# Context steps dealt out anew among the expert sets, and the column tiles of a round issued in reverse

## The chip, the core and the metric

The kernel runs on one core of one Trainium2 chip. The metric is the device time of one execution in microseconds (us); of the kernel before, three runs and one further, profiled execution are known. TensorE (PE in the rows) multiplies, its weight loads are PEld; VectorE is DVE, ScalarE is ACT, GpSimd is POOL, and SP is SyncE, whose queue issues nearly all loads from HBM. TensorE's clock has two levels, 1.2 and 2.4 GHz; a granted clock of 1.00 in the rows means 2.4 GHz all the time.

## The reference, cut to what matters

Two transformer blocks on 256 tokens of width 1024, in float32. The first block ends in a mixture of 32 experts, of which each token uses four. The second block has two layers; it works on the tokens and on a second stream of 256 context rows. The context stream of layer 0 needs nothing of the first block.

```
def moe_ffn(h, router_w, router_b, w1, b1, w2, b2):
    logits = (xt @ router_w + router_b)
    top_v, top_e = lax.top_k(logits, TOP_K)
    ...
    def expert_block(args):
        xblk, e = args
        act = clamped_swiglu(xblk @ w1[e] + b1[e])
        return act @ w2[e] + b2[e]

def second_block(x, c, ctx, ...):
    for l in range(DEPTH_2):
        ...
        y, yc = token_mixer(h, hc, rope, need_ctx, ...)
        xl = xl + gt1 * rms_norm(y, g_post_mix[l])
        ...
        if need_ctx:
            xc = xc + cgt1 * rms_norm(yc, g_post_mix[l])
            hc = rms_norm(xc, g_pre_ffn[l]) * (1.0 + csc2) + csh2
            xc = xc + cgt2 * rms_norm(swiglu(hc, w_ffn_in[l], w_ffn_out[l]), g_post_ffn[l])
```

The weights of one expert are w1 (1024 x 2048) and w2 (1024 x 1024), 12.6 MB together; all 32 experts are read, 403 MB.

## The kernel before, in words

The program is written as generators. `run` drives the first block, then the experts (`moe`), and beside the experts a second generator, `cside`: layer 0 of the context stream, cut into steps. A step takes one tile `raw` of 1 MB of weights from HBM, cuts its two halves into a high and a low part (`split`: ACT writes `wh` at L363, DVE writes `wl` at L364) and issues 48 matmuls on 256 columns into the PSUM bank `ps_c` (`fm` at L384 to L386, `tm` at L407 to L409, `tm2` at L433 to L435). What the step's result needs (attention, a convolution, norms, gates) follows in the same step or is spread over the next ones.

The experts are sorted by their number of tokens and worked in twelve sets: four quads (four experts, 32 column places each, list `QUADS`), six pairs (two experts of 64 places) and two mixed sets (96 and 32 places, cut into four column tiles of 32 by `w`). A column tile is a part of TensorE's columns with a stationary operand of its own (`xg`, the gathered tokens) and the PSUM partitions that belong to it; the expert's weights are the moving operand. A set has 24 rounds: eight k steps for each half `hf` of w1 (L1154, into `ps_a`) and eight for w2 (L1179, into `ps_b`). In a round each column tile (`parts`) gets two matmuls of 512 columns; in the trace each of them is two records. A round of a quad needs 2 MB of weights, loaded as four transfers of 512 KB (L1129) into two tiles `raw`; a pair or a mixed set loads whole tiles of 1 MB for each expert (L1118) and makes two rounds of them, so that a round needs 1 MB. A set ends with the matmuls at L1198, which bring its result to `acc`.

What sets the order: each round ends with `yield credit`, and `drive` adds the credits up; whenever the sum reaches 1, one context step is issued at that place of the program. The context stream may run to 74 steps here (`CTX_STEPS - REST`); then nothing more is dealt out. Behind the program's own order a scheduler decides how the instructions that are near each other stand on each engine; every engine, and the queue of SP, then works strictly in that order. Two rings of buffers matter: the seven tiles of 1 MB for the experts' weights (`RAW = 7`) and a ring of its own for the context's weights while the experts run (`rawx`), which holds one tile; so a context load can't be issued before the step ahead of it has been split.

Of the kernel before, what the change touches and what calls it, by code (L numbers as in the profile page):

```python
# [28 lines left out]
for _s in SETS:  # L29
    for _r, _o, _m in _s:  # L30
        CAPS[_r] = _m
CREDIT = {1: 0.0, 2: 0.5, 4: 0.4}
NEG = 1e30
HEADS = 16
CONVW = 31
# [257 lines left out]
class _Kernel:  # L293
# [839 lines left out]
    def experts(self, tp, rawp, es, rs, xg, b1, sel, ct, acc, mid=None, first=None):  # L1133

        V, S, T, A = self.V, self.S, self.T, self.A
        n = len(es)
        parts = []

        w = 32 if any(m != rs[0][2] for _, _, m in rs) else rs[0][2]
        for i, (_, o, m) in enumerate(rs):  # L1140
            parts += [(slice(c, c + w), i) for c in range(o, o + m, w)]
        credit = CREDIT[n] if n == 4 else CREDIT[n] / 2
        aT = tp.tile([128, 8, 128], F32, name="aT", tag="aT", bufs=1)
        for hf in range(2):
            pg = self.bank("a")
            pl = self.bank("a")
            for j, ps in enumerate((pg, pl)):
                T.matmul(ps, sel[:, 2 * hf + j], b1, start=True, stop=False)
            k = 0
            for kc in range(4):  # L1150
                for ws in self.weights(rawp, A["w1"], es, hf * 4 + kc):
                    for ps, o in ((pg, 0), (pl, 512)):
                        for c, i in parts:
                            T.matmul(ps[c], xg[:, k, c], ws[i][:, o:o + 512],  # L1154
                                     start=False, stop=(k == 7), tile_position=(0, c.start))
                    k += 1
                    if k < 8:
                        yield credit
            t = tp.tile([128, 512], F32, name="et", tag="et", bufs=1)
            g, l = pg, pl  # L1160
            V.tensor_scalar(g, pg, 7.0, None, op0=OP.min)  # L1161
            S.activation(t, g, AF.Tanh, scale=0.851)  # L1162
            V.tensor_scalar(l, pl, 7.0, -7.0, op0=OP.min, op1=OP.max)
            V.scalar_tensor_tensor(t, t, 1.0, g, op0=OP.add, op1=OP.mult)
            V.scalar_tensor_tensor(t, l, 1.0, t, op0=OP.add, op1=OP.mult)
            pt = self.pst()
            for f in range(4):
                T.transpose(pt[:, f * 128:(f + 1) * 128], t[:, f * 128:(f + 1) * 128], self.ident)
            S.activation(aT[:, hf * 4:hf * 4 + 4, :], pt.rearrange("p (f n) -> p f n", f=4), AF.Copy, scale=0.5)
            yield credit  # L1170
        if mid is not None:
            mid()
        py = [self.bank("b") for _ in range(2)]
        f = 0
        for fc in range(4):
            for ws in self.weights(rawp, A["w2"], es, fc):
                for h in range(2):
                    for c, i in parts:
                        T.matmul(py[h][c], aT[:, f, c], ws[i][:, h * 512:(h + 1) * 512],  # L1179
                                 start=(f == 0), stop=(f == 7), tile_position=(0, c.start))  # L1180
                f += 1
                if f < 8:
                    yield credit
        y = tp.tile([128, 1024], F32, name="ey", tag="aT", bufs=1)
        for h in range(2):
            S.activation(y[:, h * 512:(h + 1) * 512], py[h], AF.Copy)
        for a in range(2):
            for h in range(2):
                ps = self.pst()
                hs = slice(h * 512, (h + 1) * 512)  # L1190
                if first is not None:

                    gT, (b2,) = first
                    T.matmul(ps, gT[:, a * 128:(a + 1) * 128], b2[0:NE, hs], start=True, stop=False)
                    T.matmul(ps, ct[:, a, :], y[:, hs], start=False, stop=True)
                    S.activation(acc[:, a, hs], ps, AF.Copy)
                    continue
                T.matmul(ps, ct[:, a, :], y[:, hs], start=True, stop=True)  # L1198
                V.tensor_add(acc[:, a, hs], acc[:, a, hs], ps)
        yield credit  # L1200
# [662 lines left out]
```

## Time and profile before

| | before |
|---|---|
| median of 3 runs | 2876.57 us (2874.08 to 2879.45) |
| profiled execution, its own time | 2880.69 us |
| its span, first to last instruction | 2878.9 us |
| PE, PEld, DVE, ACT busy | 94%, 70%, 50%, 38% of the span |
| mean granted clock | 0.981 |
| read from HBM | 780.74 MB, 274 GB/s over the span |

The busy shares are means over stages with different limits, and a busy TensorE holds time in which a matmul record covers a wait behind it. What the change can be worth is therefore read set by set, between the ends of the twelve expert sets, which lie between 367 and 1725 us.

### The profile page before, as it was taken

To read this page: it belongs to the slowest core of one execution; us is meant where nothing else is said; L and a number is where in the kernel's file an instruction comes from. 1 tells how busy PE (TensorE), PEld (TensorE's weight loads), DVE (VectorE), ACT (ScalarE), POOL (GpSimd) and SP (SyncE) were. 2 spreads that over 40 slices of the span, in tenths; PEclk is the share of its full clock that TensorE was granted. 3 is DMA by queue.
4 is the path that set the end of the run, shared out by engine and by line. 5 is a ranking of instruction groups with operands and counts; after the bars stand their busy time and mean duration, and the time that the engine had idled before them with its cause. 6 is when DMAs were issued, how large, how long until landed. Compare 5 with 4: busy or idle time off the path is not lost. (4 is left out here: it accounts for less than half of the span.)

```text
span 2878.9 us, 47309 instructions
## 1 busy us (share of the span) xinstructions
PE 2710.6 (94%) x19078; PEld 2022.1 (70%) x19078; DVE 1439.7 (50%) x2413; ACT 1093.0 (38%) x1970; POOL 194.8 (7%) x305
## 2 busy tenths in 40 slices
PE   6999999989899999999999998999999999999998
PEld 4888854555554556555655337788989997889998
DVE  3974653253223333323332116886665658866655
ACT  3653522322123222212221115555644455556443
POOL 1110100000000000000000002220000021300000
PEclk8999999989999999999999999999999999999999
DMA  8768678999999998888788996445766563345452
GB/s 335 265 264 331 236 274 317 343 349 397 378 392 358 396 366 326 336 330 323 311 338 337 405 413 229 147 161 211 252 221 234 201 214 125 113 159 183 156 189 74
DMA packets 145406, 790.94 MB, mean 275 GB/s; under 512 B 16832, under 2 KB 18880, under 8 KB 78112
## 3 DMA queue, kind: packets, MB, share of 16 engines
q1 hardware_dynamic: 141056, 773.46, 70.4%
q0 software_dynamic: 4128, 14.42, 1.3%
q8 instruction: 151, 2.47, 0.3%
q14 instruction: 71, 0.58, 0.1%
HBM read 780.74 MB, written 7.08 MB: 274 GB/s over the span
## 5 line engine op out<-in xcount | busy, mean ns | idle before, releaser
L364 DVE TENSOR_TENSOR wl<-raw,wh 128x1024 fp32r<-128x1024 f32 (+1 forms) x542 | 653.9, 1219 | 550.2 <-ACT wh L363 533.2
L363 ACT ACTIVATE wh<-raw 128x1024 fp32r<-128x1024 f32 (+1 forms) x542 | 558.9, 1047 | 656.0 <-PE ps_a L385 311.4
L384 PE MATMUL ps_a<-hh,wh 128*128 128x256 f32 x1888 | 543.3, 288 | 7.2 <-ACT wh L363 3.9
L385 PE MATMUL ps_a<-hl,wh 128*128 128x256 f32 x1888 | 532.7, 282 | 0.4 <-DVE hl L534 0.2
L386 PE MATMUL ps_a<-hh,wl 128*128 128x256 f32 x1888 | 532.5, 282 | 0.6 <-DVE wl L364 0.6
L1154 PE MATMUL ps_a<-raw,xg 128*32 128x512 f32 (+1 forms) x2304 | 441.1, 599 | 3.8 <-DMA raw<-in_w_dram 3.6
L384 PEld LDWEIGHTS ps_a<-hh,wh 128*128 128x128 f32 x1888 | 359.3, 190 | 53.7 <-issue 37.7
L385 PEld LDWEIGHTS ps_a<-hl,wh 128*128 128x128 f32 x1888 | 359.1, 190 | 3.0 <-DVE wl L364 1.4
L386 PEld LDWEIGHTS ps_a<-hh,wl 128*128 128x128 f32 x1888 | 358.7, 190 | 3.1 <-DVE wl L364 2.6
L1154 PEld LDWEIGHTS ps_a<-raw,xg 128*32 128x32 f32 (+1 forms) x2304 | 124.2, 119 | 243.4 <-issue 211.6
L384 PE MATMUL ps_c<-hh,wh 128*128 128x256 f32 x832 | 246.4, 296 | 17.4 <-ACT wh L363 17.2
L386 PE MATMUL ps_c<-hh,wl 128*128 128x256 f32 x832 | 245.7, 295 | 11.3 <-DVE wl L364 11.3
L385 PE MATMUL ps_c<-hl,wh 128*128 128x256 f32 x832 | 238.9, 287 | 0.0
L1179 PE MATMUL ps_b<-raw,aT 128*32 128x512 f32 (+1 forms) x1152 | 215.4, 597 | 1.0 <-DMA raw<-in_w_dram 1.0
L384 PEld LDWEIGHTS ps_c<-hh,wh 128*128 128x128 f32 x832 | 162.3, 195 | 53.0 <-ACT wh L363 35.2
L386 PEld LDWEIGHTS ps_c<-hh,wl 128*128 128x128 f32 x832 | 162.4, 195 | 37.3 <-DVE wl L364 26.2
L385 PEld LDWEIGHTS ps_c<-hl,wh 128*128 128x128 f32 x832 | 162.3, 195 | 5.3 <-issue 5.3
L1677 DVE SCALAR_TENSOR_TENSOR wv<-u,cw,wv 128x256 f32<-128x256 f32 x360 | 163.9, 496 | 1.3 <-ACT wv L1674 0.7
L1179 PEld LDWEIGHTS ps_b<-raw,aT 128*32 128x32 f32 (+1 forms) x1152 | 59.7, 118 | 115.8 <-issue 105.1
L1161 DVE TENSOR_SCALAR ps_a<-ps_a 128x512 f32<-128x512 f32 x24 | 16.8, 700 | 193.8 <-PE ps_a L1154 193.8
L454 PE MATMUL ps_c<-raw,st 128*32 128x512 f32 x576 | 84.2, 608 | 2.1 <-DMA raw<-in_w_ada_dram 2.1
L1162 ACT ACTIVATE et<-ps_a 128x512 f32<-128x512 f32 x24 | 14.3, 597 | 189.0 <-DVE ps_a L1161 188.9
(506 smaller groups left out, 4486.8 us busy)
## 6 DMA issues: line engine op xcount, KB each, us to landing
raw<-in_w_dram SPq DMA_DIRECT2D x384, 512.0 KB, 10.3
raw<-in_w_dram SPq DMA_DIRECT2D x192, 1024.0 KB, 9.4
raw<-in_w_in_dram SPq DMA_DIRECT2D x120, 1024.0 KB, 5.1
raw<-in_w_f_dram SPq DMA_DIRECT2D x66, 1024.0 KB, 4.9
raw<-in_w_mod_dram SPq DMA_DIRECT2D x48, 1024.0 KB, 5.7
raw<-in_w_ada_dram SPq DMA_DIRECT2D x24, 1024.0 KB, 8.4
raw<-in_w_y_dram SPq DMA_DIRECT2D x24, 1024.0 KB, 6.3
raw<-in_w_f2a_dram SPq DMA_DIRECT2D x24, 1024.0 KB, 4.9
```

Of the source, the lines that this page charges most:

```text
L363: s = self.S.activation(h[:, :n], src, AF.Copy)
L364: self.V.tensor_sub(l[:, :n], src, h[:, :n].bitcast(F32))
L384: self.T.matmul(o, wh[:, w], ah, start=(k == 0), stop=False)
L385: self.T.matmul(o, wh[:, w], al, start=False, stop=False)
L386: self.T.matmul(o, wl[:, w], ah, start=False, stop=(k == kt - 1))
L454: self.T.matmul(ps[32 * j:32 * j + 32, :], st[:, k, :], raw[:, 512 * j:512 * (j + 1)], start=(k == 0), stop=(k == 7), tile_position=(0, 32 ...
L1154: T.matmul(ps[c], xg[:, k, c], ws[i][:, o:o + 512], start=False, stop=(k == 7), tile_position=(0, c.start))
L1161: V.tensor_scalar(g, pg, 7.0, None, op0=OP.min)
L1162: S.activation(t, g, AF.Tanh, scale=0.851)
L1179: T.matmul(py[h][c], aT[:, f, c], ws[i][:, h * 512:(h + 1) * 512], start=(f == 0), stop=(f == 7), tile_position=(0, c.start))
L1677: return V.scalar_tensor_tensor(wk, u[:, f, j:j + 256], cw[:, j * 4 + k:j * 4 + k + 1], wk, op0=OP.mult, op1=OP.add)
```

## The change

Two things in `experts` and the table above it. The credit of a round was 0.4 in a quad and 0.25 in a pair or mixed set (`CREDIT[2] / 2`); it is now 0.6 and 0.07. And the list of a round's column tiles is reversed, so that the tile whose expert's weights are loaded last is issued first.

```
-CREDIT = {1: 0.0, 2: 0.5, 4: 0.4}
+CREDIT = {1: 0.0, 2: 0.07, 4: 0.6}
...
         for i, (_, o, m) in enumerate(rs):
             parts += [(slice(c, c + w), i) for c in range(o, o + m, w)]
-        credit = CREDIT[n] if n == 4 else CREDIT[n] / 2
+
+        parts.reverse()
+        credit = CREDIT[n]
```

How it moves instructions, first on ACT, in the third quad, from the Tanh of the first half of w1 (L1162, two lines lower in the changed kernel) to that of the second half, eight rounds later. Before:

```order
L1162 ACTIVATE et<-ps_a 128x512
L363 ACTIVATE wh<-raw 128x1024
L1169 ACTIVATE aT<-ps_t 128x512
L363 ACTIVATE wh<-raw 128x1024 x3
L1416 ACTIVATE tg<-ps_c,hbg 128x256 x2
L363 ACTIVATE wh<-raw 128x1024 x2
L1416 ACTIVATE tg<-ps_c,hbg 128x256 x2
L1162 ACTIVATE et<-ps_a 128x512
```

The same place in the changed kernel, where the context stream is at later steps:

```order
L1164 ACTIVATE et<-ps_a 128x512
L363 ACTIVATE wh<-raw 128x1024 x2
L1171 ACTIVATE aT<-ps_t 128x512
L1418 ACTIVATE tg<-ps_c,hbg 128x256 x2
L363 ACTIVATE wh<-raw 128x1024 x2
L1418 ACTIVATE tg<-ps_c,hbg 128x256 x2
L363 ACTIVATE wh<-raw 128x1024 x2
L1563 ACTIVATE mh<-m 128x512 x4
L363 ACTIVATE wh<-raw 128x1024 x2
L557 ACTIVATE rjk,rst<-ps_c 128x256 x2
L363 ACTIVATE wh<-raw 128x1024 x2
L557 ACTIVATE rjk,rst<-ps_c 128x256 x2
```

Six splits, the weights of three context steps, stand between the two halves before, and ten, those of five steps, in the change.

On ACT in one of the later pairs, `aT` and `et` being the expert's own work and `ah`, `fs`, `y` the context's feed-forward. A stretch of a pair before, from behind one set's end to the second half's transpose:

```order
L363 ACTIVATE wh<-raw 128x1024 x2
L1365 ACTIVATE y<-ps_c 128x2x256
L1162 ACTIVATE et<-ps_a 128x512
L363 ACTIVATE wh<-raw 128x1024 x2
L1169 ACTIVATE aT<-ps_t 128x512
L1343 ACTIVATE fs<-ps_c 128x512
L363 ACTIVATE wh<-raw 128x1024 x2
L1348 ACTIVATE ah<-fs 128x512
L1162 ACTIVATE et<-ps_a 128x512
L363 ACTIVATE wh<-raw 128x1024 x2
L1169 ACTIVATE aT<-ps_t 128x512
```

A whole pair of the change, from the first half's Tanh to the set's end (L1188):

```order
L1164 ACTIVATE et<-ps_a 128x512
L1171 ACTIVATE aT<-ps_t 128x512
L363 ACTIVATE wh<-raw 128x1024 x2
L1164 ACTIVATE et<-ps_a 128x512
L1171 ACTIVATE aT<-ps_t 128x512
L1094 ACTIVATE xg<-ps_t,modT,A_3548 128x128 x8
L1188 ACTIVATE ey<-ps_b 128x512 x2
```

Where a pair had the splits of four steps in the rows of two thirds of it, it now has those of one in the whole.

On PE in a quad, where a context step begins (`oh`, `hh` are the step's activations). Before:

```order
L1154 MATMUL ps_a<-raw,xg 32x512 x23
L384 MATMUL ps_c<-oh,wh 128x256
L385 MATMUL ps_c<-ol,wh 128x256
L1154 MATMUL ps_a<-raw,xg 32x512
L386 MATMUL ps_c<-oh,wl 128x256
L384 MATMUL ps_c<-oh,wh 128x256
```

In the change:

```order
L386 MATMUL ps_c<-hh_8578,wl 128x256
L1156 MATMUL ps_a<-raw,xg 32x512 x16
L384 MATMUL ps_c<-hh_8578,wh 128x256
L385 MATMUL ps_c<-hl_8579,wh 128x256
L386 MATMUL ps_c<-hh_8578,wl 128x256
```

The scheduler drew the first column tile of the next round, whose weights come first, into the context step, away from the other seven matmuls of its round; reversed, the rounds stand whole (16 is two rounds of eight).

## Rows read from the trace of the kernel before

**Rows 1.** Windows, one for each expert set (four quads, six pairs, two mixed).

```profile
core 0: us, PE busy (x) PEld busy (x) DVE busy (x) ACT busy (x) POOL busy (x), PEclk, DMA share, GB/s
367.00:565.00 198.00, 189.58 (x1046) 102.75 (x1044) 76.59 (x192) 60.09 (x158) 9.35 (x14) 0.97 0.90 324
565.00:720.00 155.00, 137.94 (x920) 83.86 (x920) 67.70 (x136) 43.93 (x91) 3.52 (x8) 0.93 0.97 366
720.00:883.00 163.00, 152.12 (x943) 88.97 (x942) 43.39 (x61) 32.46 (x50) 11.17 (x22) 0.96 1.01 387
883.00:1054.00 171.00, 154.85 (x979) 92.88 (x978) 55.56 (x77) 46.53 (x77) 1.54 (x3) 0.98 0.96 375
1054.00:1152.00 98.00, 91.65 (x522) 54.78 (x522) 35.03 (x58) 29.22 (x51) 2.56 (x5) 0.98 0.81 330
...
1442.00:1539.00 97.00, 92.52 (x540) 56.49 (x540) 29.45 (x41) 21.78 (x32) 0.75 (x2) 1.00 0.81 327
1539.00:1604.00 65.00, 61.31 (x298) 28.43 (x296) 13.69 (x25) 7.12 (x15) 0.74 (x2) 1.00 0.91 368
1604.00:1666.00 62.00, 57.92 (x442) 21.87 (x442) 8.19 (x14) 6.49 (x14) 0.75 (x2) 1.00 1.00 412
1666.00:1725.00 59.00, 53.74 (x407) 17.91 (x405) 8.69 (x13) 6.39 (x10) 0.00 (x0) 1.00 1.01 417
```

**Rows 2.** The same windows, ACT's splits at L363 alone: the four quads.

```profile
367.00:565.00 198.00, 14.98 (x15) 0.97 0.90 324
565.00:720.00 155.00, 19.86 (x20) 0.93 0.97 366
720.00:883.00 163.00, 18.15 (x18) 0.96 1.01 387
883.00:1054.00 171.00, 22.22 (x22) 0.98 0.96 375
```

**Rows 3.** The same windows, matmuls into `ps_c` alone: the last two pairs.

```profile
1442.00:1539.00 97.00, 38.15 (x288) 1.00 0.81 327
1539.00:1604.00 65.00, 6.22 (x48) 1.00 0.91 368
```

**Rows 4.** DMA of the four quads, 367 to 1054 us: total, and one issue line.

```profile
DMA packets 62513, 248.28 MB, mean 361 GB/s; under 512 B 6975, under 2 KB 6975, under 8 KB 57311
...
raw<-in_w_in_dram SPq DMA_DIRECT2D x23, 1024.0 KB, 10.3
```

**Rows 5.** PE's timeline in the third quad: start, us, instructions.

```profile
731.69 1.04 PE L1154 MATMUL ps_a<-raw,xg 128*32 128x512 f32 x2
732.67 0.39 PE L386 MATMUL ps_c<-hh,wl 128*128 128x256 f32 x1
```

**Rows 6.** PE's timeline in the first quad.

```profile
393.27 1.90 PE L1154 MATMUL ps_a<-raw,xg 128*32 128x512 f32 x4
...
440.36 1.92 PE L1154 MATMUL ps_a<-raw,xg 128*32 128x512 f32 x8
```

**Rows 7.** PE's timeline in a pair.

```profile
1182.57 7.09 PE L1154 MATMUL ps_a<-raw,xg 128*64 128x512 f32 x32
1189.58 0.38 PE L384 MATMUL ps_c<-hh,wh 128*128 128x256 f32 x1
...
1195.41 7.14 PE L1154 MATMUL ps_a<-raw,xg 128*64 128x512 f32 x32
```

**Rows 8.** Waits of SP's queue in the quads, 367 to 1054 us: total, times, longest.

```profile
SPq L352 <- DVE wl L364: 57.3, 16, 11.6
```

**Rows 9.** DVE's and SP's timelines in the second quad.

```profile
575.18 14.47 DVE L1677 SCALAR_TENSOR_TENSOR wv<-u,cw,wv 128x256 f32<-128x256 f32 x36 [0.73 <-ACT wv L1674]
589.57 2.35 DVE L364 TENSOR_TENSOR wl<-raw,wh 128x1024 fp32r<-128x1024 f32 x2
591.95 0.34 SPq L352 DMA_DIRECT2D raw<-in_w_in_dram  x1
```

**Rows 10.** The window of 580 to 600 us, columns as in rows 1.

```profile
580.00:600.00 20.00, 10.64 (x62) 8.58 (x66) 20.00 (x48) 2.42 (x4) 0.29 (x1) 0.66 0.69 271
```

## The prediction

> **What bounds the kernel now.** I read the windows of the twelve expert sets first, since the change touches nothing else: from 367 to 1725 us, 1358 of the 2878.9 us. In [rows 1] the reader is to see two kinds of set beside each other. In the quads the DMA share is 0.90 to 1.01 and PE's busy time lies below the window's length: there the transfers bound. In a full pair the DMA share is 0.81 and PE is busy for 92.5 of 97 us: there TensorE bounds, and a fifth of the DMA engines' time is left unused. The mixed sets, which carry no context step (the stream's 74 steps have run out by then), run at 412 and 417 GB/s, which is what the DMA engines give when nothing holds them up.
>
> Rate times length over all twelve windows is 481 MB (the three pairs left out of [rows 1] are counted like the one at 1442): 248.1 MB in the quads, 183.1 in the pairs, 50.1 in the mixed sets. At 412 GB/s that would be 1167 us; the stretch takes 191 us more. Of these the quads lose 687 - 248.1/0.412 = 85 us, the six pairs 550 - 183.1/0.412 = 106 us.
>
> What the quads lose is seen in the waits of SP's queue and in one place of the second quad. A context load waits for the split of the step ahead of it, 57.3 us in 16 waits [rows 8]. At 575 us DVE works through 36 convolution taps in a row, the split stands behind them, and the next context load goes out at 591.95 [rows 9]; the weights behind it in SP's queue wait too, and the DMA share of 580 to 600 us is 0.69 [rows 10].
>
> What the pairs lose is plain work of TensorE. A context step's 48 matmuls take 5.83 us (1189.58 to 1195.41, [rows 7]), and a full pair has six of them (288 matmuls into `ps_c`), the last pair one (48) [rows 3]. The full pair takes 97 us, the last one 65: 32/5 = 6.4 us for a step. Without any, a pair's time would be near the mixed sets' 62.
>
> **The change part by part.** *Credits.* A quad gets 24 x 0.6 = 14.4 steps in place of 9.6, a pair or mixed set 24 x 0.07 = 1.68 in place of 6. With the four steps dealt out ahead of the sets' own rounds that is 4 + 57.6 + 13.4 = 75, so the limit of 74 is reached in the last set, and nothing is left to be done behind it. No transfer and no matmul is added or taken away; 19 steps go from the pairs to the quads, some two of them on to the mixed sets.
>
> The pairs: 6 x 1.68 = 10.1 steps, and one more that spills over from the last quad. From the 65 us of the pair with one step, and 6.4 us for each further one: 6 x 65 + (11.1 - 6) x 6.4 = 423 us in place of 550, **-127**. Bounds: if the transfers alone counted, 6 x (25.2 + 1.87 x 1.05) MB / 0.412 = 395 us, -155; if the pair without steps were 97 less six times the bare 5.83 us, 62 + 1.87 x 5.83 = 73 us each, 438 us, -112. I take the step between two measured sets.
>
> The mixed sets get about 2.3 steps while the transfers bound them: 2.3 x 1.05 MB / 0.412 = **+6**; if TensorE became their bound, 2.3 x 5.83 = +13; nothing, if the steps hid wholly.
>
> The quads: the splits counted there are 15, 20, 18 and 22, two a step [rows 2], so 30 steps in the last three quads, 43.2 after. 13.2 x 1.05 = 13.9 MB more. At the rate those three have now, 183.9 MB in 489 us = 376 GB/s, this is 37 us. The first quad is the one in which TensorE is nearly the bound (189.6 of 198 us busy): about 6 steps more are 6 x 5.83 = 35 us, against which the broken rounds go (next), 26 us; +9. Together **+46**. Bounds: all four at the third quad's 387 GB/s, 268/0.387 = 693, +6; at 412 GB/s 651, -36. The other way, if the 85 us lost in the quads grew with the number of steps (37.5 by the splits, 2.27 us each, to 57), 651 + 57 x 2.27 = 780, +93. I stay nearest the present rate because what is lost belongs to places of the context stream (the taps, the norms), which pass once whatever the density, and most of the steps that move in come from the feed-forward, which has few such places.
>
> *Reversed column tiles.* The transfers of a round land one behind the other; its last matmul can't start ahead of the last landing in either order, so a round that waits ends at the same time. What the reversal changes is where a context step cuts a round. Before, the first column tile of the next round stands alone in the step: 731.69 to 732.67, 0.98 us for one matmul [rows 5], while four rounds of a pair, 16 matmuls, take 7.09 us [rows 7], 1.8 us for a whole round. The other seven or three matmuls take their two turns all the same, so each lone tile costs about 1 us. In the quads outside the first one the transfers hide it. In a pair I count one or two; the base of 65 us holds one, so six pairs give 6 x 1.0 and something of the step's 6.4: **-7**. Bounds 0 and -10. In the first quad it is more: between 393 and 442 us, 40 matmuls, five rounds, go in 14 pieces of 1.83 to 1.92 us [rows 6] in place of five times 1.8: 17 us, and nine lone tiles elsewhere in that quad 9: the 26 us used above.
>
> The cover under which the cost in the quads lies is the queue of transfers ahead. Between two context loads SP now issues 2.5 rounds, 5.2 MB or 12.7 us at 412 GB/s; after the change 1.67 rounds, 3.5 MB or 8.5 us. A context load takes 10.3 us to land [rows 4] because it stands behind others; then come the splits, 2.35 us of DVE for both halves [rows 9]. SP will therefore stand at most context loads, but the transfers behind the first go on meanwhile. What is late next, if a split is held up by more than some 8 us, is the expert weights; the 14.47 us of taps would cost 4 us more than now.
>
> The sum: -127 + 6 + 46 - 7 = **-82 us**. The profiled execution took 2880.69 us (span 2878.9 and 1.8 around it), 4.1 over the median of the runs shown; 82 off the median gives 2794.6, which I round to **2795 us**.
>
> **One rule weighed.** In the rows the transfers reach 412 and 417 GB/s in the mixed sets [rows 1], so the 361 GB/s of the quads [rows 4] is no ceiling. The Trainium skill, DMA: Bandwidth & Descriptors, section Bandwidth, says that for transfers from HBM the memory side binds, at about 358 GB/s a core, though it also measures 425 with one core streaming. By the first figure the 481 MB would need 1343 us, and the change could gain 15 at most; by the rows it has up to 191 to gain. The measurement decides, and I give that ceiling no chance.
>
> **The rivals.** *The quads run freer* (0.14). More steps ahead of the waiting rounds, and rounds left whole, could let the transfers reach 412 GB/s there: -36 in the quads and the pairs near their lower bound, -36 - 140 + 3 = -173 at the end, 2704; usually part of it, 2710 to 2755. For it: the third quad already has 387. Against: the taps and norms stay.
>
> *The loss goes with the steps* (0.16). +93 in the quads, -127 + 6 - 7 elsewhere: -35, 2842. For it: the one buffer for context weights, and the shorter 8.5 us between its loads. Against: the quad with the most splits (22) has 375 GB/s, the one with the fewest 324.
>
> *Slower* (0.04): the same buffer stops SP oftener and longer. It decides from the point where the quads take 687 + 128 = 815 us, that is (815 - 651)/57 = 2.9 us lost for each step against 2.27 now. If each step met the wait of 3.6 us that is the mean of the sixteen, all of it with the transfers standing, the quads would take 651 + 57 x 3.6 = 856 us, +41 in sum, 2918. Against: with all those waits in them the last three quads show DMA shares of 0.96 to 1.01 [rows 1].
>
> *The clock* (0.01). With few steps between them, the pairs' rounds will wait for transfers with gaps; if TensorE then ran at 1.2 GHz, a round would take 1.8 us more, 24 x 8 x 1.8 = 346 us, and a quarter of the rounds would eat the gain. The mixed sets, which have just these gaps, were granted 1.00, the quads 0.92 to 0.98 [rows 1]. The Trainium skill, TensorE: Matmul & The Clock Gate, HAM oscillation, tells of kernels whose clock falls in waits for each tile's transfer. The mixed sets show no such fall.
>
> *No change that can be measured* (0.03): the losses of the quads just eat what the pairs gain. 0.2%, 6 us, is about what a measurement of this kernel can tell from none.
>
> My forecast, 2755 to 2830, has the remaining 0.62. Range: 2740 to 2845 takes in the lower part of the second and nearly all of the third case; below it lies about 0.07, above it about 0.12. Faster by more than 0.2%: 0.92; within: 0.03; slower: 0.05.
>
> **What would show it.** Right: full pairs of 66 to 73 us at a DMA share over 0.9, quads of 165 to 185 us with 14 steps each (first quad 195 to 215), no lone matmul of a round ahead of a context step, mixed sets still near 412 GB/s. Wrong, if the quads pass 200 us with SP waiting at L352 and DMA shares under 0.8, if pairs stay over 80 us, or if the granted clock in pairs falls under 0.95. What lies outside 367 to 1725 us should keep its length.

## The result, and the profile after

The changed kernel takes 2844.48 us (median of 4 runs, 2840.63 to 2847.49) against 2875.32 us of the kernel before in the same comparison: a ratio of 0.9895, 95% interval 0.9882 to 0.9907. It is faster by 31 us where 82 were forecast. The profiled execution took 2847.49 us, its span is 2845.7.

Windows of the twelve sets of the changed kernel: the four quads, the first and the last pair, the two mixed sets. They answer to [rows 1]; the columns are the same.

```profile
366.00:598.00 232.00, 202.35 (x1321) 132.41 (x1319) 122.56 (x289) 84.12 (x217) 12.91 (x18) 0.92 0.81 302
598.00:775.00 177.00, 153.40 (x1142) 107.74 (x1141) 53.27 (x76) 45.34 (x68) 10.31 (x22) 0.96 0.92 349
775.00:971.00 196.00, 160.80 (x1164) 114.18 (x1163) 76.59 (x108) 63.72 (x107) 3.65 (x8) 0.92 0.92 349
971.00:1144.00 173.00, 144.85 (x1113) 100.55 (x1112) 51.99 (x64) 42.35 (x56) 0.74 (x2) 0.98 0.98 374
1144.00:1219.00 75.00, 71.21 (x388) 36.99 (x387) 19.32 (x32) 12.38 (x21) 0.75 (x2) 1.00 0.98 402
...
1489.00:1560.00 71.00, 65.82 (x339) 30.84 (x338) 14.47 (x27) 9.51 (x18) 0.75 (x2) 1.00 0.95 387
1560.00:1630.00 70.00, 66.14 (x539) 30.75 (x538) 15.36 (x21) 11.74 (x20) 0.74 (x2) 1.00 0.97 395
1630.00:1689.00 59.00, 51.90 (x413) 16.12 (x412) 9.61 (x15) 6.53 (x10) 0.00 (x0) 0.97 1.00 405
```

The pairs fell from 97 us to 64 to 75, with a DMA share of 0.95 or more. The quads grew from 198, 155, 163 and 171 us to 232, 177, 196 and 173. By kind of set: pairs 550 to 416 us, mixed sets 121 to 129, quads 686 to 778; the rest of the program 1521 and 1523 us.

The same windows of the changed kernel, ACT's splits at L363 alone, in the quads (beside [rows 2]): 110 in place of 75, two a step.

```profile
366.00:598.00 232.00, 24.82 (x24) 0.92 0.81 302
598.00:775.00 177.00, 28.29 (x28) 0.96 0.92 349
775.00:971.00 196.00, 30.17 (x30) 0.92 0.92 349
971.00:1144.00 173.00, 28.04 (x28) 0.98 0.98 374
```

DMA of the changed kernel's quads, 366 to 1144 us, and the first line of the waits of SP's queue there; they answer to [rows 4] and [rows 8].

```profile
DMA packets 65024, 265.08 MB, mean 341 GB/s; under 512 B 7249, under 2 KB 7249, under 8 KB 57841
```

```profile
SPq L352 <- DVE wl L364: 228.5, 49, 18.3
```

16.8 MB more are transferred there, 41 us at 412 GB/s. The rest is loss: 687 - 248.28/0.412 = 84 us before, 778 - 265.08/0.412 = 135 after. SP stands at a context load (L352) for 228.5 us in place of 57.3, because the only tile for context weights has not been split yet (`wl`).

One such place, in the first quad of the changed kernel. DVE's timeline, then SP's, then two windows.

```profile
406.22 22.26 DVE L1679 SCALAR_TENSOR_TENSOR wv<-u,cw,wv 128x256 f32<-128x256 f32 x56
...
437.05 2.45 DVE L364 TENSOR_TENSOR wl<-raw,wh 128x1024 fp32r<-128x1024 f32 x2 [4.60 <-ACT wh L363]
```

```profile
416.17 9.33 SPq L1129 DMA_DIRECT2D raw<-in_w_dram  x8
439.52 0.34 SPq L352 DMA_DIRECT2D raw<-in_w_in_dram  x1
440.14 2.04 SPq L1129 DMA_DIRECT2D raw<-in_w_dram  x4
457.62 0.34 SPq L352 DMA_DIRECT2D raw<-in_w_in_dram  x1
```

```profile
430.00:440.00 10.00, 8.79 (x40) 3.85 (x41) 4.90 (x7) 2.49 (x3) 2.00 (x4) 0.74 0.48 184
...
450.00:460.00 10.00, 8.31 (x54) 4.96 (x53) 5.55 (x12) 6.21 (x20) 1.71 (x1) 1.00 0.12 31
```

SP issues nothing from 425.5 to 439.5; it issues one round, 2 MB, and stands again from 442.2 to 457.6. The transfers run dry: 184 and 31 GB/s. The way from the taps to the late split goes over ACT's timeline:

```profile
429.12 0.60 ACT L1164 ACTIVATE et<-ps_a 128x512 f32<-128x512 f32 x1 [7.00 <-DVE ps_a L1163]
435.47 0.60 ACT L1171 ACTIVATE aT<-ps_t 128x512 f32<-128x512 f32 x1 [5.75 <-PE ps_t L1170]
435.96 2.00 ACT L363 ACTIVATE wh<-raw 128x1024 fp32r<-128x1024 f32 x2
```

The expert's own work on DVE (L1163) stands behind the 56 taps, so ACT waits 7.00 us for it and then 5.75 us for TensorE, which needs the result; ACT's part of the split (L363) stands behind both, and DVE's part waits for that. The Trainium skill, Perfetto Trace Analysis, Tensor Engine Instruction, says beside TensorE's reordering that DVE and ACT work strictly in order; these rows agree.

PE's timeline of the changed kernel in the last pair, around its one place where a context step starts behind a round.

```profile
1512.17 10.62 PE L1156 MATMUL ps_a<-raw,xg 128*64 128x512 f32 x48
1524.15 3.65 PE L1156 MATMUL ps_a<-raw,xg 128*64 128x512 f32 x16 [1.37 <-DMA raw<-in_w_dram]
1527.74 0.39 PE L384 MATMUL ps_c<-hh,wh 128*128 128x256 f32 x1
```

The rounds stand whole (48 and 16 records, eight a round); no lone matmul is left ahead of the step, unlike [rows 5].

### The profile page after: what moved, and what is told of

Same layout as the page of the kernel before. It is cut to its first block, busy times and chain, and to the rows that moved or that the text cites. A ratio compares the mean times of both kernels' runs of the same rounds, so it can differ in the third digit from the quotient of the medians.

```text
span 2845.7 us, 47285 instructions
## 1 busy us (share of the span) xinstructions
PE 2613.3 (92%) x19078; PEld 1992.8 (70%) x19078; DVE 1441.7 (51%) x2413; ACT 1093.8 (38%) x1970; POOL 192.0 (7%) x305
## 5 line engine op out<-in xcount | busy, mean ns | idle before, releaser
L363 ACT ACTIVATE wh<-raw 128x1024 fp32r<-128x1024 f32 (+1 forms) x542 | 560.1, 1049 | 664.7 <-PE ps_a L385 309.6
L1156 PE MATMUL ps_a<-raw,xg 128*32 128x512 f32 (+1 forms) x2304 | 356.5, 604 | 22.7 <-DMA raw<-in_w_dram 22.7
L1156 PEld LDWEIGHTS ps_a<-raw,xg 128*32 128x32 f32 (+1 forms) x2304 | 96.5, 119 | 233.4 <-issue 187.2
L1181 PE MATMUL ps_b<-raw,aT 128*32 128x512 f32 (+1 forms) x1152 | 179.1, 609 | 5.0 <-DMA raw<-in_w_dram 5.0
L1181 PEld LDWEIGHTS ps_b<-raw,aT 128*32 128x32 f32 (+1 forms) x1152 | 48.6, 120 | 105.9 <-issue 94.0
L1163 DVE TENSOR_SCALAR ps_a<-ps_a 128x512 f32<-128x512 f32 x24 | 16.8, 700 | 185.2 <-PE ps_a L1156 185.2
```

Of the source, the lines that this page charges most:

```text
L363: s = self.S.activation(h[:, :n], src, AF.Copy)
L1156: T.matmul(ps[c], xg[:, k, c], ws[i][:, o:o + 512], start=False, stop=(k == 7), tile_position=(0, c.start))
```

## The experiments

Two theories stood at the start. **The gate** (theory 1 in the expectations): the one tile of context weights (`rawx`) stops SP's queue, and the expert weights behind the load with it. **The places**: the loss belongs to heavy places of the context stream (the taps, attention, norms) or is simply the added transfers, whatever the number of tiles. Two more were tried beside them: that rounds issued in reverse make the quads slow (theory 2), and that TensorE's order is the bound in dense quads, SP's standing only following from it (theory 3). Another, **the pace**, came later. Sums over the sets are read between the last matmuls of each set (the first quad from its first matmul on), from the profiled run of each kernel; medians and ratios (against the kernel before on the same chip) follow. The runs come from several chips, on which the kernel before has medians of 2872.7 to 2877.8 us, so a difference of 5 us between two medians of the table tells nothing.

| kernel | quads | pairs | mixed | median us | ratio, 95% interval |
|---|---|---|---|---|---|
| before | 686 | 550 | 121 | 2875.32 | 1 |
| changed | 778 | 416 | 129 | 2844.48 | 0.9895, 0.9882 to 0.9907 |
| old credits, reversed | 680 | 533 | 122 | 2857.28 | 0.9941, 0.9919 to 0.9964 |
| new credits, not reversed | 798 | 418 | 128 | 2854.68 | 0.9922, 0.9902 to 0.9941 |
| six tiles, two for context | 751 | 422 | 134 | 2831.80 | 0.9846, 0.9822 to 0.9869 |
| six tiles, one for context | 779 | 422 | 136 | 2862.81 | 0.9959, 0.9948 to 0.9971 |
| before, six and two | 703 | 550 | 125 | 2908.33 | 1.0124, 1.0103 to 1.0145 |
| context tile in halves | 767 | 414 | 130 | 2821.48 | 0.9804, 0.9782 to 0.9826 |
| all through the ring of 7 | 744 | 416 | 132 | 2814.36 | 0.9800, 0.9784 to 0.9817 |
| alternating | 747 | 416 | 129 | 2810.17 | 0.9777, 0.9757 to 0.9798 |
| context loads on ACT's queue | 846 | 420 | 120 | 2909.89 | 1.0131, 1.0104 to 1.0157 |
| without 29 taps | 765 | 416 | 129 | 2827.25 | 0.9841, 0.9820 to 0.9861 |
| credits 0.5, 0.12 | 685 | 457 | 138 | 2794.57 | 0.9723, 0.9707 to 0.9739 |
| the same, alternating | 683 | 457 | 139 | 2802.38 | 0.9756, 0.9740 to 0.9773 |
| credits 0.8, 0 | 844 | 364 | 122 | 2852.52 | 0.9917, 0.9890 to 0.9944 |
| the same, alternating | 789 | 362 | 120 | 2789.06 | 0.9696, 0.9669 to 0.9723 |
| credits by quad | 739 | 427 | 137 | 2823.26 | 0.9808, 0.9781 to 0.9835 |
| the same, alternating | 718 | 427 | 137 | 2802.76 | 0.9742, 0.9721 to 0.9763 |
| old credits, alternating | 682 | 534 | 121 | 2858.52 | 0.9947, 0.9928 to 0.9966 |

**The two parts of the change alone.** The changed kernel without the reversal, and the kernel before with it.

```
-        parts.reverse()
...
+        parts.reverse()
```

> The new credits without the reversal of the column tiles. Theory 1 (the quads lost what they did because SP's queue stands at the context loads, for whose weights there is one tile): the reversal has little part in it; the quads stay within 10 us of the changed kernel's 778 us, the pairs lose about 7 us by lone column tiles, 2845 to 2857 us in all. Theory 2 (the reversed rounds, which wait for their last transfer before any of their matmuls starts, are what makes the quads slow): quads of 750 us or less, under 2835 us.

> The old credits with the column tiles reversed. Theory 1: the reversal only takes lone column tiles away, 2 in each of five full pairs at 1 us and the broken rounds of the first quad: 10 to 30 us faster than before, 2845 to 2865 us, the full pairs at 94 to 96 us. Theory 2: the quads get longer than 687 us, and the whole is slower than 2880 us.

The reversal alone gives 2877 x 0.0059 = 17 us, with pairs of 93 to 95 us in place of 96 to 98; with the new credits it gives 10 of the medians, and in the profiled runs, which differ by 14, 19 in the quads and 2 in the pairs. The credits alone give 2877 x 0.0078 = 22. In both kernels the reversal shortens the quads, so theory 2 is out; that the quads would stay within 10 us without it was missed too.

**A second tile for context weights**, with six tiles for the experts in place of seven; as controls the six tiles alone, and both in the kernel before.

```
-RAW = 7
+RAW = 6
...
-            self.pc.raws = es2.enter_context(p.pool("rawx"))
+            self.pc.raws = es2.enter_context(p.pool("rawx", 2))
```

> The changed kernel with two tiles for context weights beside the experts and six in place of seven for the experts' own (SBUF has no room for one more). Theory 1: SP's waits at context loads for the split fall from 228 us in the quads to under 80, the quads from 778 to 700 to 735 us, the whole to 2785 to 2815 us; the tile taken from the experts costs under 10 us. Theory 3 (with 14 steps in a quad TensorE's order, rounds and context matmuls in one queue, is the bound, and SP's standing only follows from it): the same time as the changed kernel within 10 us, 2835 to 2855.

> The changed kernel with six tiles for expert weights and one for context weights: the control for the kernel with six and two. Theory 1: the missing tile costs the quads and the pairs something, 2850 to 2870 us, so that the second context tile by itself is worth 20 to 40 us. If it costs nothing (2840 to 2849), the second tile is worth only the 13 us seen.

> The kernel before with six tiles for expert weights and two for context weights. Theory 1: with 2.5 rounds between context loads the single tile hurts little (57 us of waits in the quads, covered by transfers ahead), so the second tile gives 0 to 15 us in the quads, and the pairs, bound by TensorE, nothing: 2860 to 2880 us. If the second tile gave as much as in the changed kernel or more (under 2855), density would not be the point.

The first line of the waits of SP's queue in the quads, with two context tiles and then with one.

```profile
SPq L1129 <- PE ps_a L1156: 161.9, 43, 8.7
```

```profile
SPq L352 <- DVE wl L364: 186.8, 48, 13.2
```

With the second tile SP waits for the experts' own rounds, and the quads take 28 us less (779 to 751), the kernel 31, which theory 3 does not allow for; it is less than expected (quads of 700 to 735), and most of the loss stays. The seventh tile is worth 18 us at the new credits, none of it in the quads, where under 10 were expected. At the old credits six and two are slower than the kernel before (quads of 703 us, 2908 in all, where 2860 to 2880 were expected); six tiles and one were not run there, so the second tile by itself is not priced by it. The old credits come back below.

**Other ways past the gate**: the context tile as two halves of 512 KB, each loaded and freed by itself; no tile of its own, so that context loads go through the ring of seven; and loads that take turns between the two.

```
+            t = pool.tile([128, 1024], F32, name="raw", tag="raw")
+            self.nc.sync.dma_start(t[:, :n], src[:, j:j + n])
...
-            self.pc.raws = es2.enter_context(p.pool("rawx"))
...
+            self.turn = not self.turn
+            return self.load(src, p.raws if self.turn else self.rawp)
```

> The changed kernel with the one tile for context weights cut into two halves of 512 KB, loaded apart, so that a half is loaded again as soon as its own split is done, in the same room of SBUF. Theory 1: SP stands less long at each context load, its waits there fall from 228 us to 100 to 170, the whole gets 10 to 35 us faster, 2810 to 2835 us. Theory 3: no change beyond 8 us.

> The changed kernel without a tile of its own for context weights: they go through the ring of seven that the expert weights use, so there is one tile less in all, but a context load no longer has to wait for the split of the step just ahead. Theory 1 (the gate of the one tile is what costs the quads some 50 us at 14 steps): waits for splits vanish at context loads, the quads gain 20 to 40 us on the changed kernel's 778 us, 2805 to 2835 in all. If only the amount of room counted, it would be slower than the changed kernel, over 2850.

> The changed kernel with context loads going in turn to the one tile of their own and to the ring of seven: two places for context weights at no cost in room, and all seven tiles for the experts half of the time. Theory 1: quads of 735 to 755 us (750.8 with six and two), pairs as in the changed kernel (416 us), 2800 to 2825 in all.

All three are faster than the changed kernel, by 23, 30 and 34 us, as expected. The waits of SP's queue in the quads, alternating, first line and one further down (the numbers of its lines are six higher):

```profile
SPq L1135 <- PE ps_a L1162: 162.0, 44, 9.9
...
SPq L1135 <- PE ps_t L1202: 21.0, 1, 21.0
```

No wait for `wl` stands among the long ones, but the quads still take 747 us, 104 more than 265 MB at 412 GB/s. The single wait of 21.0 us is taken up below.

**Context loads on ACT's queue**, so that a load that waits holds no expert weights back in SP's queue.

```
-        self.nc.sync.dma_start(t[:r, :n], src)
+        eng = self.nc.sync if pool is None or pool is self.rawp else self.nc.scalar
+        eng.dma_start(t[:r, :n], src)
```

> The changed kernel with the context loads issued from ACT's queue in place of SP's while the experts run; still one tile for them. It parts two halves of theory 1. 1a (the expert weights suffer because they stand behind the context load in SP's queue): SP no longer waits for a split at all, the quads gain at least as much as with two tiles, 735 to 755 us, the whole 2800 to 2830. 1b (the context steps themselves come late, and TensorE waits for them in its own order): SP's waits move to TensorE's freeing of tiles, the quads stay at 765 to 785 us, the whole at 2835 to 2855.

It is slower than the kernel before, outside both expectations, and it decides nothing, since a new wait took the old one's place. Waits of SP's queue in its quads:

```profile
SPq L1130 <- DMA raw<-in_w_in_dram: 167.7, 21, 11.8
SPq L1130 <- DMA raw<-in_w_f_dram: 128.5, 13, 13.2
```

SP, which no longer issues the context loads, now waits at the experts' loads until context loads have landed. Why the two were tied together was not tried.

**The taps.** 29 of the 30 convolution taps of the context stream are left out, so a part of its computation is missing.

```
-                for j in range(1, CONVW):
+                for j in range(1, 2 if c["own"] else CONVW):
```

> The changed kernel without 29 of the 30 taps that DVE adds for each quarter of the context stream's convolution (that part of the computation is left out). If the long runs of taps on DVE, behind which the splits stand, are what stops SP in the first two quads, these lose 20 to 40 us of their 409, and the whole is at 2805 to 2825 us; SP's waits for splits in the quads fall from 228 to about 190 us. If the taps are only where the wait is seen, under 8 us.

14 us of the quads go, less than the 20 to 40 expected, all in the first one (232 to 217), and 17 of the median; 7 of the 15 us in the first quad lie in one step at its end, of which more below. The wait for `wl` in the quads remains, 200.2 us in 49 waits. The taps lengthen some waits; they are not the cause of most.

**Fewer steps in the quads**, with the reversal, and with one context tile or alternating.

```
-CREDIT = {1: 0.0, 2: 0.07, 4: 0.6}
+CREDIT = {1: 0.0, 2: 0.12, 4: 0.5}
```

> The changed kernel with credits between the old and the new (0.5 in quads, 0.12 in pairs and mixed sets): 12 steps in a quad, 2.9 in a pair. Pairs by the measured 6.4 us a step: 416 + 6 x 1.2 x 6.4 = 462 us. Theory 1 with a threshold (the wait begins where the rounds between context loads, 8.5 us at 0.6 and 10.2 us at 0.5, are shorter than a load and its splits): quads at or under 730 us, 2825 to 2845 in all. If the loss goes evenly with the steps: quads at 742, 2850 to 2862.

> The kernel with context loads in turn to their own tile and to the ring, at credits 0.5 and 0.12. Theory 1: with the gate gone the quads hardly care for density, so fewer steps in them only put work back into the pairs at 6.4 us against 2.5 us for their transfers: slower than the same kernel at 0.6 and 0.07 by 5 to 25 us. If it is faster than that one, the quads still lose by density in another way.

With one tile: 2794.57 us, 50 faster than the changed kernel. Windows of its quads, and the first line of SP's waits there:

```profile
366.00:560.00 194.00, 168.11 (x1144) 109.21 (x1144) 107.16 (x256) 66.97 (x166) 11.04 (x15) 0.92 0.91 332
560.00:723.00 163.00, 142.93 (x1068) 98.36 (x1067) 51.95 (x87) 48.69 (x96) 14.11 (x25) 0.96 1.00 386
723.00:884.00 161.00, 141.48 (x1037) 97.26 (x1035) 60.94 (x89) 51.02 (x81) 1.81 (x5) 0.95 1.00 395
884.00:1051.00 167.00, 141.15 (x1058) 98.11 (x1057) 58.33 (x82) 46.39 (x78) 2.57 (x5) 0.95 0.99 390
```

```profile
SPq L352 <- DVE wl L364: 117.2, 37, 9.1
```

With twelve steps in a quad in place of nine to eleven the quads take no longer than before (685 us), though SP stands 117 us at the gate. Both are far under the 730 us that a threshold was thought to allow. Opening the gate changes nothing there (683; the median is 8 us higher, which the sums of the sets don't show). I had expected the alternating loads to lose some us against 0.6 with them; they gained 8. So a credit of 0.6 is too much for the quads with or without the gate: with it open, 64 us lie between 0.5 and 0.6, of which the added transfers are 22 and the rest was left without a cause.

**The pace.** From the 4th to the 40th context step (counted by 48 matmuls into `ps_c`) the stream took 626 us at 0.4, 510 at 0.5 and 500 at 0.6: as if the stream itself needed some 14 us a step from 0.5 on. More steps still, all dealt out in the quads, with one tile and alternating, had to show it.

```
+CREDIT = {1: 0.0, 2: 0.0, 4: 0.8}
```

> The changed kernel with 0.8 a round in the quads and none in the pairs: 1.25 rounds between two context steps in place of 1.67. Measured so far from the 4th to the 40th step: 626 us at 0.4 (92 rounds), 510 at 0.5 (73.5), 500 at 0.6 (61.4). Theory of the pace (above 0.5 the context stream itself takes 13 to 14 us a step, and a round less between steps saves 0.9 to 1.8 us): 16 rounds fewer, 470 to 485 us; the quads some 990 us, the pairs 60 each, about 2995 us in all. Rival, the loss goes with the steps while the transfers bound (5.1 us a round, 2.55 a context load, 2.3 lost at each): 403 to 416 us, the quads about 800, 2810 in all.

> The same 0.8 with context loads that alternate between their own tile and the ring of seven, so that no load waits for the split of the step just ahead. From the 4th to the 40th step this took 513 us at 0.5 and 480 at 0.6, 2.7 us for a round less. Theory of the pace (without the gate too; a limit in the stream's own work): 436 to 450 us, the quads about 895, 2900 in all. Rival, without the gate the transfers bound: 396 us, the quads about 780, 2790 in all.

The pace falls. The 36 steps took 417 us with one tile and 394 alternating, 11.6 and 10.9 a step: the rivals' numbers. With one tile the quads took 844 us, though, 44 more than the rival gave. Windows of the second to fourth quad and the first pair, alternating:

```profile
593.00:791.00 198.00, 181.16 (x1388) 133.45 (x1386) 83.78 (x117) 70.40 (x110) 14.78 (x23) 0.98 0.96 368
791.00:988.00 197.00, 177.51 (x1381) 132.91 (x1381) 75.51 (x98) 60.47 (x91) 3.82 (x7) 0.98 0.95 360
988.00:1155.00 167.00, 143.12 (x1062) 93.81 (x1061) 51.97 (x65) 35.41 (x47) 1.73 (x2) 0.93 1.00 383
1155.00:1215.00 60.00, 54.62 (x251) 20.60 (x250) 10.20 (x22) 6.48 (x14) 0.74 (x2) 1.00 0.99 409
```

The first two hold 19 steps each. The pairs without steps take 60 us, and the kernel, 2789.06 us, is as fast as the one with 0.5 and one tile: with the gate open, 0.5, 0.6 and 0.8 lie within 21 us (2802, 2810 and 2789).

**Credits by the quad**, 0.5, 0.6, 0.5, 0.6 and 0.09 for the pairs, with one tile and alternating.

```
+QUAD = [0.5, 0.6, 0.5, 0.6]
...
+        credit = self.quad.pop(0) if n == 4 else CREDIT[n]
```

> Credits by the quad, 0.5, 0.6, 0.5, 0.6 and 0.09 for the pairs, with the one tile for context weights. 4.8 steps leave the pairs and mixed sets against 0.5 for all, 29 us. Theory of the pace (the costly steps are those in the first and third quad): quads 193 + 177 + 161 + 173 = 704, so 2795 + 20 - 29 = 2786 us. Rival (density as such, 23 us for each quad at 0.6): 731, 2812 us.

> The same credits by the quad with alternating context loads. Theory of the pace: quads 190 + 170 + 163 + 160 = 683, as with 0.5 for all, and 29 us less in the pairs: 2802 - 29 = 2773 us, faster than every kernel so far. Rival (density as such, 16 us for each quad at 0.6): 715, 2805 us.

Quads of 739 and 718 us, near the rival's 731 and 715: the loss comes with the density in the second and fourth quad too, not only where the heavy steps are (20 and 27 us more there than with 0.5 for all on one tile, 7 and 17 alternating). The third quad, whose credit stayed at 0.5, took 9 and 11 us more as well, for which no cause was found.

**The gate at the old density**: the old credits, reversed, with alternating loads.

```
-CREDIT = {1: 0.0, 2: 0.07, 4: 0.6}
+CREDIT = {1: 0.0, 2: 0.25, 4: 0.4}
```

> The old credits (0.4 in the quads, 0.25 in pairs and mixed sets), reversed tiles, context loads that alternate between their own tile and the ring of seven. To be compared with the old credits and reversed tiles on the one tile (2857 us, quads 680 us). With and without the gate the quads took 685 and 683 us at 0.5, 778 and 747 at 0.6, 844 and 789 at 0.8. If the gate costs only where the rounds between two context loads are short, it costs nothing here: quads 675 to 683, about 2855 us. If each context load loses a like time at it, some 0.6 to 0.8 us for 39 steps: quads 650 to 657, about 2830 us.

682 us in the quads, against 680 with one tile, as expected of a gate that costs only at short distances.

**Taken together.** What the gate costs in the quads, as the difference between one tile and alternating loads, against the rounds between two context loads and their time at 412 GB/s (2.097 MB a round):

| credit | rounds | us | quads, one tile | alternating | gate |
|---|---|---|---|---|---|
| 0.4 | 2.5 | 12.7 | 680 | 682 | -2 |
| 0.5 | 2.0 | 10.2 | 685 | 683 | 2 |
| 0.6 | 1.67 | 8.5 | 778 | 747 | 31 |
| 0.8 | 1.25 | 6.4 | 844 | 789 | 55 |

The price begins between 10.2 and 8.5 us of other transfers between two context loads. Where they last longer, SP's wait is hidden by the transfers it has issued already, even 117 us of it: the longest single wait was 11.6 us in the kernel before, at 0.4 ([rows 8]), and 9.1 at 0.5, shorter than the transfers between two loads. At 0.6 the longest was 18.3 us, and six went over 8.5; at 0.8 it was 11.7:

```profile
SPq L352 <- DVE wl L364: 261.4, 57, 11.7
```

What single waits go over the transfers between two loads is less than the price (23 us in sum at 0.6, 10 of them in the place that follows), so the comparison gives the threshold and not the price. At 0.8 alternating loads still wait for `wl`, 79.1 us in the quads, so the 55 are not all of it.

A second part of the loss at 0.6 is one place. The 16th context step (the end of attention, with `w_y`) took 19.7 us before, 22.2 at 0.5, and 37.3 in the changed kernel, with two rounds in it each time. At this density it meets the end of the first quad. The group of L1197 there in the changed kernel, a window, and SP's timeline:

```profile
L1197 PE MATMUL ps_t<-ey,ct x8: 973/1061/1223, 585.1 to 597.8; 128*128 128x512 f32 x8
```

```profile
590.00:600.00 10.00, 10.00 (x17) 3.64 (x16) 0.00 (x0) 2.26 (x4) 0.00 (x0) 0.50 0.00 0
```

```profile
578.04 0.34 SPq L352 DMA_DIRECT2D raw<-in_w_y_dram  x1
578.64 2.37 SPq L1129 DMA_DIRECT2D raw<-in_w_dram  x4
603.93 0.34 SPq L352 DMA_DIRECT2D raw<-in_w_in_dram  x1
```

The end of the first set is a block of matmuls (L1196, L1197) and of ACT's evictions to `acc` behind each; the splits of the step stand behind them, SP issues nothing from 581.0 to 603.9, and the transfers stop (0 GB/s). The step lost 17.5 us more than before, counted as its time less its transfers at 412 GB/s (24.5 against 7.0). Alternating, it lost 24.3: there SP stands 21.0 us because a tile of the ring is held by L1202, the same matmuls (the single wait in the alternating kernel's rows above). With 0.5 it lost 9.5 with either, and at 0.8 with one tile, where it ends 42 us ahead of the set's end, 7.0: what it costs goes by the place and not by the density.

So of the 92 us by which the quads grew, 41 are the added transfers, 31 the gate (28 by the second tile) and about 17 this meeting; 3 are left. Against the quads at 0.5 (loss 685 - 256.0/0.412 = 64 us) the changed kernel loses 71 more: the gate 29, the meeting 15, and 27 at other steps, which alternating loads do not give back. That part stays open; at 0.5 a step falls on every second round, at 0.6 on the second, the second and the next one, which may be it, but was not tried by itself; nor is it excluded that TensorE's order (theory 3) has a share in it.

## Why the prediction was right in direction and wrong in size

- *Pairs, -127, and mixed sets, +6*: right. 550 to 416 us is -134, without the reversal -132; the mixed sets +8. That the sum of the pairs' two terms, -134, came out to the us is luck: the reversal's 7 were not there, and a step cost less than the 6.4 us read between two sets. Pairs took 60 to 61 us without a step (at 0.8), 64 to 65 with one, 70 to 71 with two, some 5.5 us a step, near the bare 5.83.
- *Reversed tiles, -7*: the count was 33 in truth, these 7 and the 26 taken off in the quads' term for the first quad. The reversal gave 10 by the medians with the new credits and 17 with the old. The first quad got only 8 us shorter at the old credits (198 to 190) and 2 at the new (234 to 232); some of its rounds still go in pieces (4 of 16 records at 450.06 us). At the old credits 17 us are in the pairs, over 3 in each full one, although in the pair from 1152 to 1248 us of the kernel before only two of the six steps cut a round, as I had counted; what gave the rest stays open.
- *Quads, +46*: this step failed; they took 92 more, the first 34 in place of 9, the other three 58 in place of 37. The transfers were 41 us for 16.8 MB. What failed is "I stay nearest the present rate because what is lost belongs to places of the context stream (the taps, the norms), which pass once whatever the density": the loss grew from 84 to 135 us, 31 by the gate and 17 by the one meeting. The sentence on the cover failed with it: SP "will therefore stand at most context loads, but the transfers behind the first go on meanwhile". It held at 10.2 us between loads and no longer at 8.5. I had the 8.5 us and the landing of 10.3 beside each other, named only a split held up by more than 8 us, 4 us for the taps, and left even these out of the sum. Of the signs named, the second and fourth quad came (177 and 173 us); the first and third, 232 and 196, did not.
- *The rival that the loss goes with the steps* gave +93 and 2842 us, and its numbers came true; its rule did not. At 0.5 there were 47 steps in the quads in place of 39 and 64 us of loss in place of 84. The loss has a threshold, and one place of its own.
- *The rivals of a freer quad, of a slower kernel and of the clock*: none came. The pairs were granted 1.00; the gaps feared there hardly came, the 1.37 us in the row above being the only wait of a round for its transfer that their rows show. The Trainium skill, TensorE: Matmul & The Clock Gate, HAM oscillation, tells of a kernel whose clock falls in a wait for the transfer of each tile; with one wait in six pairs, these rows don't test it.
- *The ceiling*: the first pair moved 402 GB/s, over the 358 that the Trainium skill, DMA: Bandwidth & Descriptors, Bandwidth, gives as the limit of HBM for a core, and under the 425 that it measured with one core alone; the measurement decides again.
- *Outside the sets* nothing changed, as forecast: 1521 and 1523 us.

## What to carry to other kernels

A load that may wait for a buffer, in a queue that works in order, cost nothing here as long as the transfers between two such loads lasted longer than its longest wait: compare these two times, and keep the density under the point where they meet or add a second buffer. Four densities in one kernel show this; the price beyond that point was not found from the waits. The length of the wait alone doesn't tell the price: 117 us cost nothing here, 228 cost 31. When work is dealt out by a table, look also at what each heavy step will stand beside, since one meeting with a set's end cost as much as half the gate.

## What the runs showed of the hardware that was not expected

- In the block at the end of the first quad TensorE was granted 0.50, the lower level, from 590 to 600 us, and its 16 matmuls took 1.06 us each at the median in place of 0.64 in the kernel before. In the 8 us ahead of it, 576 to 584, TensorE had been busy for 7.05 us with short matmuls, at 1.00. With all loads through the ring of seven it was busy for the same 7.05 us ahead of the block (573 to 581), and the block kept 1.00 and took 8.5 us in place of 14.9; why the clock fell in the one and not in the other is not shown. The block also kept 1.00 without the reversal, where the step lost 19.4 us, and without the taps, where it lost 17.4, in place of 24.5: of the meeting some 5 to 7 us are the clock.
- Moved to another queue, the context loads were waited for by SP, up to 13.2 us at a time, and the kernel lost 65 us against the changed one.
